# One load of x split between two DMA queues: 12 KB of fifteen rows through GpSimd's, 12 KB of a sixteenth in sixteen pieces

## The chip, the cores and the metric

The kernel runs on one core of a Trainium2 chip. The metric is the device time in microseconds (us) from launch to end; a time is the median of several executions, and one further execution was recorded by the hardware profiler. Lower is better.

## What is computed

The reference is a low-rank update of a residual stream. Input `x` has 16 x 512 = 8192 tokens of 768 float32 values, `A` is 768 x 16, `B` is 16 x 768:

```python
lora = np.matmul(np.matmul(x, A), B)
return (x + scale * lora).astype(np.float32)   # scale = 0.5
```

So 25.2 MB of `x` have to be read and 25.2 MB of output written; `A` and `B` are 48 KB each.

## The kernel before, in words

**Tiling.** The tokens lie in five parts of 8, 8, 16, 16 and 16 tokens per partition (`PARTS`, L14); a part of S tokens takes S x 128 rows of `x`, and partition p holds S rows that follow one another in memory. A partition's share of one load is therefore one run of bytes, 3 KB per token: 48 KB for the load of a part of 16. All of `x` but the last part has its own room in on-chip memory (`x_all`, L62); the last part takes the room of the first two, once these are stored. The result is summed into `x_all` in place and stored from there.

**Loads and stores.** `LOADS` (L106) cuts the five parts into eight loads, numbered 0 to 7; `STORES` (L129) has five. All of them, and those of `A` (three DMAs of four rows of 4 KB, L156) and `B` (one DMA of 16 rows of 3 KB, L160), are issued by SyncE (`on_sync`, L136), in this order: loads 0 and 1, `A`, `B`, loads 2 to 5; then stores 0 and 1; load 6 when store 0 has landed, load 7 when store 1 has landed; then stores 2 and 3, and store 4 at L356. Before store 2 SyncE waits until TensorE has begun its sixth pass over `raised(0)` (`s_raise`, L182). Each load has a semaphore of its own (`s_load`), which reaches 16 when all of the load has landed. **Load 5** is the one that the change touches: part 3, 16 tokens, 6144 KB, 48 KB on each of the 128 partitions. It is the largest of the loads.

**Compute.** Tokens go in groups of 8 (`GROUP`), half a group (`SUB` = 4) at a time through the narrowing to float16 (`narrowed`, L188): ScalarE takes the first half of every group, GpSimd the second. VectorE transposes the group in 32 x 32 blocks (L255), TensorE multiplies by `A` (L285), ScalarE spreads the product into a block-diagonal tile (`y_bd`, L240), TensorE multiplies by `B` (L306), and VectorE adds the product to `x` in place (L260), two tokens at a time. The engines' programs are written out by hand, with semaphores; nothing is planned by a scheduler inside this section.

**GpSimd** (`on_gpsimd`, L200) begins with memsets and the mask `pick`, narrows the first two tokens of group 0 (load 0), waits for `B` (L213), narrows it (`b_half`, L214), waits for the transposed `A`, and builds the weights (`w_one`, `w_bd`, L216 to L225). Then it narrows the second half of groups 1 to 7 (L226). Group 4 is tokens 0 to 7 of load 5, group 5 its tokens 8 to 15; GpSimd reads tokens 12 to 15 of it in group 5.

Of the kernel before, what the change touches and what calls it, by code (L numbers as in the profile page):

```python
# [16 lines left out]
GROUP = 8  # L17

SUB = 4
# [9 lines left out]
def kernel(  # L29
# [9 lines left out]
    fp32 = mybir.dt.float32  # L39
    P = 128  # L40
# [3 lines left out]
    x2 = x.flatten_outer_dims()  # L44
# [10 lines left out]
    def sb(name, shape, dtype):  # L55
        return nc.alloc_sbuf_tensor(name, shape, dtype).ap()

    def ps(name, shape):
        return nc.alloc_psum_tensor(name, shape, fp32).ap()
# [15 lines left out]
    xn = sb("xn", [P, GROUP, D], MM_DT)  # L75
    xt = sb("xt", [P, GROUP, D], MM_DT)
    y_bd = sb("y_bd", [P, GROUP, P], MM_DT)
    lora = [ps(f"lora_ps{i}", [P, 2, D]) for i in range(2)]
    y_ps = ps("ps_yt", [P, GROUP, Q])

# [2 lines left out]
    def sem(name):  # L83
        sems.append(nc.alloc_semaphore(name))
        return sems[-1]
# [3 lines left out]
    where = []  # L89
# [6 lines left out]
    def memory(t2, i, s, n):  # L96
        S = PARTS[i]
        return t2[ds(parts[i], S * P), :].rearrange("(p s) d -> p s d", s=S)[:, ds(s, n), :]

    def held(i, s, n):  # L100
        return tiles(where.index((i, s)), n)

    def tiles(t, n):
        return x_all[:, ds(t % ROOM, n), :]

    LOADS = [  # L106
        (0, 0, 2), (0, 2, 6), (1, 0, 8), (2, 0, 8), (2, 8, 8), (3, 0, 16), (4, 0, 8), (4, 8, 8)
    ]
    s_load = [sem(f"s_load{k}") for k in range(len(LOADS))]

    def load_of(t):
        i, s = where[t]
        return next(k for k, ld in enumerate(LOADS) if ld[0] == i and ld[1] <= s < ld[1] + ld[2])
# [9 lines left out]
    s_out0, s_out1, s_raise = sem("s_out0"), sem("s_out1"), sem("s_raise")  # L123


    s_sum, s_out = tc.alloc_semaphore("s_sum"), tc.alloc_semaphore("s_out")

    MMS = 2 * NC
# [6 lines left out]

    def on_sync(e):  # L136
        def load(k):
            ld = LOADS[k]
            e.dma_start(out=held(*ld), in_=memory(x2, *ld)).then_inc(s_load[k], 16)  # L139

        def summed(k):
            e.wait_ge(s_sum, k + 1)
            if STORED[k] + 1 < NG:

                e.sem_inc(s_free[PAIRS - 1], 1)

        def store(k, done):
            st = STORES[k]
            e.dma_start(out=memory(out2, *st), in_=held(*st)).then_inc(done, 16)

        load(0)
        load(1)
        e.wait_ge(s_ready, 1)
        blocks = A.rearrange("(c e) r -> c (e r)", e=64)
        for c in range(SETS):
            e.dma_start(  # L156
                out=a_rows[c : SET * SET : SET, :], in_=blocks[ds(c * SET, SET), :]
            ).then_inc(s_a, 16)
        e.wait_ge(s_brows, 1)
        e.dma_start(out=b_rows[0 : R * APART : APART, :], in_=B).then_inc(s_b, 16)  # L160
        for k in range(2, len(LOADS) - 2):
            load(k)

        for p in range(2, PAIRS):
            e.sem_inc(s_free[p], 1)
        summed(0)
        summed(1)


        e.wait_ge(s_lora, 2 * PAIRS + 2)  # L170
        store(0, s_out0)
        store(1, s_out1)
        e.wait_ge(s_out0, 16)
        load(len(LOADS) - 2)
        e.wait_ge(s_out1, 16)
        load(len(LOADS) - 1)
        for k in range(2, len(STORES)):
            summed(k)
            if k == 2:


                e.wait_ge(s_raise, 6)  # L182
            if k + 1 < len(STORES):
                store(k, s_out)
# [3 lines left out]
    def narrowed(e, copy, g, first, n=SUB):  # L188
        t = g * GROUP + first
        for k in dict.fromkeys(load_of(t + k) for k in range(n)):  # L190
            if (e, k) not in here:
                here.add((e, k))
                e.wait_ge(s_load[k], 16)
        if g:
            e.wait_ge(s_taken, g)
        ins = copy(out=xn[:, ds(first, n), :], in_=tiles(t, n))  # L196

        ins.then_inc(s_narrow if g else s_first if first else s_a, 1)

    def on_gpsimd(e):  # L200
        e.memset(a_rows[0:Q], 0.0).then_inc(s_ready, 1)  # L201
        e.memset(b_rows, 0.0).then_inc(s_brows, 1)  # L202
        e.memset(pick, 0.0).then_inc(s_pick, 1)
        e.memset(w_bd.rearrange("p c k m -> p (c k m)").bitcast(fp32), 0.0)  # L204
        e.memset(y_bd.rearrange("p s m -> p (s m)").bitcast(fp32), 0.0).then_inc(s_ready, 1)  # L205
        e.wait_ge(s_pick, 1)
        e.affine_select(  # L207
            out=pick, in_=pick, compare_op=mybir.AluOpType.not_equal, fill=1.0, base=0,
            pattern=[[0, NQ], [-APART, Q]], channel_multiplier=1,
        ).then_inc(s_pick, 1)  # L210
        narrowed(e, e.tensor_copy, 0, 0, SUB // 2)
        e.wait_ge(s_pick, 2)
        e.wait_ge(s_b, 16)  # L213
        e.tensor_copy(out=b_half, in_=b_rows).then_inc(s_bh, 1)  # L214
        e.wait_ge(s_ready, 3)
        e.tensor_copy(  # L216
            out=w_one.rearrange("i (c e) k r -> i c e (k r)", c=SETS),
            in_=a_t[0:Q].rearrange("i k r (e c) -> i c e (k r)", c=SET)[:, 0:SETS, 0:SET, :],
        ).then_inc(s_w, 1)
        e.wait_ge(s_w, 1)  # L220
        for b in range(NQ):
            e.tensor_copy(  # L222
                out=w_bd[ds(b * Q, Q), :, :, ds(b * Q, R)], in_=w_one
            ).then_inc(s_w, 1)
            e.wait_ge(s_w, b + 2)  # L225
        for g in range(1, NG):  # L226
            narrowed(e, e.tensor_copy, g, SUB)

    def on_scalar(e):
        narrowed(e, e.copy, 0, SUB // 2, SUB // 2)  # L230
        narrowed(e, e.copy, 0, SUB)
        e.wait_ge(s_bp, 1)
        e.copy(out=b_mm, in_=lora[0][:, 0, :]).then_inc(s_bm, 1)  # L233
        for g in range(NG):
            if g + 1 < NG:
                narrowed(e, e.copy, g + 1, 0)
            e.wait_ge(s_y, g + 1)
            for b in range(NQ):
                q = ds(b * Q, Q)
                last = e.mul(out=y_bd[q, :, q], in_=y_ps[q, :, :], mul=sc)  # L240
                if b == 0 and g + 1 < NG:

                    last.then_inc(s_narrow, 1)
            last.then_inc(s_spread, 1)
# [93 lines left out]

    on_sync(nc.sync)
    on_gpsimd(nc.gpsimd)  # L340
    on_scalar(nc.scalar)
    on_vector(nc.vector)
# [53 lines left out]
```

## Time and profile before

| | us |
|---|---|
| median of three executions | 123.53 |
| lowest and highest of them | 123.52 and 123.67 |
| the profiled execution | 123.47 |
| span of its instructions on the core | 121.7 |

The profile shows five engines (PE = TensorE, DVE = VectorE, ACT = ScalarE, POOL = GpSimd, SP = SyncE) and the packets of sixteen DMA engines, which all queues share. In lists of instructions the columns are the start in us from the span's beginning, the duration in us, the engine, the source line, the operation, the written and the read tile, and in brackets the idle time before it and what ended that idle time. "DMA share" is the mean busy share of the sixteen DMA engines. The packet records of the trace give each packet's start, duration, size and queue, but not which of the sixteen engines carried it. A packet of 4 bytes is the closing one of a DMA on one engine: it raises the DMA's semaphore.

### The profile page before, as it was taken

How to read it: one execution, taken by the hardware profiler on the slowest of the kernel's cores; microseconds unless marked ns; L12 is line 12 of the kernel's file. 1: busy time of each engine (PE TensorE's matmuls, PEld its weight loads, DVE VectorE, ACT ScalarE, POOL GpSimd, SP SyncE). 2: the span in 40 equal slices, each digit the busy share in tenths (PEclk: the TensorE clock that was granted, in tenths of full speed). 3: DMA queues.
4: the chain of work that ended last, by engine and by line, in shares of the span. 5: the costliest groups of instructions: out<-in, count | busy, mean ns of one | idle time of the engine just before them, and what ended most of it. 6: DMA issues, size and time to landing. Idle time of an engine off the chain costs nothing.

```text
span 121.7 us, 889 instructions
## 1 busy us (share of the span) xinstructions
PE 50.7 (42%) x322; PEld 29.6 (24%) x322; DVE 81.7 (67%) x42; ACT 37.4 (31%) x43; POOL 28.4 (23%) x24
## 2 busy tenths in 40 slices
PE   0000239477457647745745744774674320000000
PEld 0000026243323424423423322442442110000000
DVE  0002850599999999999999989999995991000000
ACT  4003928526409313644440192733004000000000
POOL 7721638017009002604400170710000000000000
PEclk9999999999999999999999999999999995555555
DMA  3999999999998997999999999997998899799790
GB/s 65 442 418 440 444 420 428 444 420 428 477 517 355 420 517 307 452 412 436 452 396 428 460 404 436 469 517 323 452 517 388 388 517 436 339 517 452 323 517 0
DMA packets 1928, 50.43 MB, mean 414 GB/s; under 512 B 236, under 2 KB 236, under 8 KB 392
## 3 DMA queue, kind: packets, MB, share of 16 engines
q1 hardware_dynamic: 1928, 50.43, 97.0%
HBM read 25.26 MB, written 25.17 MB: 414 GB/s over the span
## 4 chain that ended last, share of the span: by engine, by line
DVE 34%; DMA 28%; PE 10%; ACT 9%; issue 1%; SPq 0%; POOLq 0%
DVE x_sb L260 22%; DMA x_sb<-in_x_dram 20%; DVE xt L255 12%; DMA out_dram<-x_sb 8%; PE ps_yt L285 6%; ACT xn L196 6%; PE lora_ps L306 3%; ACT y_bd L240 3%; SPq L139 0%; SPq L391 0%; POOLq L134 0%; POOLq L377 0%
## 5 line engine op out<-in xcount | busy, mean ns | idle before, releaser
L260 DVE TENSOR_TENSOR x_sb<-x_sb,lora_ps 128x1536 f32<-128x1536 f32 x32 | 53.7, 1734 | 1.4 <-PE lora_ps L306 1.4
L306 PE MATMUL lora_ps<-b_mm,y_bd 128*128 128x512 f16 (+1 forms) x128 | 25.0, 328 | 22.4 <-ACT y_bd L240 14.1
L196 ACT CAST xn<-x_sb 128x3072 f16<-128x3072 f32 (+1 forms) x9 | 23.4, 2609 | 35.4 <-DMA x_sb<-in_x_dram 25.7
L285 PE MATMUL ps_yt<-xt,w_bd 128*128 128x256 f16 x192 | 26.1, 288 | 12.7 <-DVE xt L255 12.7
L255 DVE STREAM_TRANSPOSE xt<-xn 128x3072 f32<-128x3072 f32 (+1 forms) x9 | 27.0, 3005 | 6.5 <-ACT y_bd L240 6.1
L196 POOL CAST xn<-x_sb 128x3072 f16<-128x3072 f32 (+1 forms) x8 | 20.7, 2586 | 44.7 <-DMA x_sb<-in_x_dram 26.2
L285 PEld LDWEIGHTS ps_yt<-xt,w_bd 128*128 128x128 f16 x192 | 18.9, 101 | 20.6 <-issue 15.8
L306 PEld LDWEIGHTS lora_ps<-b_mm,y_bd 128*128 128x128 f16 x128 | 10.6, 98 | 35.3 <-ACT y_bd L240 16.4
L240 ACT ACTIVATE y_bd<-ps_yt 32x256 f16<-32x256 f32 x32 | 12.0, 374 | 19.5 <-PE ps_yt L285 19.1
L248 DVE STREAM_TRANSPOSE a_t<-a_rows 32x1024 f32<-32x1024 f32 x1 | 1.9, 1943 | 11.3 <-DMA a_rows<-in_A_dram 11.3
L319 PE MATMUL lora_ps<-b_half,pick 128*128 128x512 f16 (+1 forms) x2 | 0.8, 500 | 12.5 <-POOL b_half L214 12.5
L319 PEld LDWEIGHTS lora_ps<-b_half,pick 128*128 128x128 f16 x2 | 0.1, 106 | 12.5 <-issue 12.5
L222 POOL COPY w_bd<-w_one 32x384 f16<-32x384 f16 x4 | 2.0, 499 | 0.2
L214 POOL CAST b_half<-b_rows 128x768 f16<-128x768 f32 x1 | 0.8, 827 | 4.6 <-DMA b_rows<-in_B_dram 4.6
L196 ACT ACT_TABLE_LOAD x1 | 1.3, 1283 | 0.9 <-PEq L377 0.9
L204 POOL MEMSET w_bd<- 128x1536 f32 x1 | 1.4, 1372 | 0.0
L201 POOL MEMSET a_rows<- 32x1024 f32 x1 | 0.9, 941 | 0.5 <-POOLq L134 0.5
L216 POOL CAST w_one<-a_t 32x384 f16<-32x384 f32 x1 | 0.8, 849 | 0.9 <-DVE a_t L248 0.9
L233 ACT CAST b_mm<-lora_ps 128x768 f16<-128x768 f32 x1 | 0.8, 798 | 0.0
L202 POOL MEMSET b_rows<- 128x768 f32 x1 | 0.7, 727 | 0.0
L205 POOL MEMSET y_bd<- 128x512 f32 x1 | 0.5, 514 | 0.0
L207 POOL TENSOR_SCALAR_AFFINE_SELECT pick<-pick 128x128 f16<-128x128 f16 x1 | 0.3, 298 | 0.0
(5 smaller groups left out, 0.6 us busy)
## 6 DMA issues: line engine op xcount, KB each, us to landing
out_dram<-x_sb SPq DMA_DIRECT2D x3, 6144.0 KB, 19.4
x_sb<-in_x_dram SPq DMA_DIRECT2D x5, 3072.0 KB, 14.6
x_sb<-in_x_dram SPq DMA_DIRECT2D x1, 6144.0 KB, 41.6
out_dram<-x_sb SPq DMA_DIRECT2D x2, 3072.0 KB, 13.8
x_sb<-in_x_dram SPq DMA_DIRECT2D x1, 2304.0 KB, 9.7
x_sb<-in_x_dram SPq DMA_DIRECT2D x1, 768.0 KB, 4.6
a_rows<-in_A_dram SPq DMA_DIRECT2D x3, 16.0 KB
b_rows<-in_B_dram SPq DMA_DIRECT2D x1, 48.0 KB, 7.5
```

The costliest lines, as they stand in the source:

```text
L196: ins = copy(out=xn[:, ds(first, n), :], in_=tiles(t, n))
L201: e.memset(a_rows[0:Q], 0.0).then_inc(s_ready, 1)
L204: e.memset(w_bd.rearrange("p c k m -> p (c k m)").bitcast(fp32), 0.0)
L214: e.tensor_copy(out=b_half, in_=b_rows).then_inc(s_bh, 1)
L222: e.tensor_copy(out=w_bd[ds(b * Q, Q), :, :, ds(b * Q, R)], in_=w_one).then_inc(s_w, 1)
L240: last = e.mul(out=y_bd[q, :, q], in_=y_ps[q, :, :], mul=sc)
L248: e.transpose(out=a_t[0:Q].rearrange("i k r c -> i (k r) c"), in_=a_rows[0:Q].rearrange("c (i k r) -> c (k r) i", k=2, r=R),).then_inc(s_r ...
L255: return e.transpose(out=ts[0], in_=ts[1])
L260: ins = e.tensor_tensor(out=xs, in0=xs, in1=lora[p % 2], op=mybir.AluOpType.add)
L285: mm = e.matmul(y_ps, w_bd[:, c, k, :], xv[:, :, c, :, k], start=(m == 0), stop=(m == MMS - 1),)
L306: mms.append(e.matmul(t[:, k, ds(n0, w)], y_bd[:, 2 * p + k, :], b_mm[:, ds(n0, w)], start=True, stop=True,))
L319: last = e.matmul(lora[0][:, 0, ds(n0, w)], pick.rearrange("p b r -> p (b r)"), b_half[:, ds(n0, w)], start=True, stop=True,)
```

## The change

Load 5 is issued as several DMAs in place of one.

- Through SyncE's queue, in place of the single DMA: partitions 0 to 111 with all 16 tokens (48 KB each); partitions 112 to 127 with tokens 0 to 11 (36 KB each); partition 127 with tokens 12 to 15 (12 KB, one run of memory that is cut into 16 pieces of 768 bytes). All three count on load 5's semaphore, so its readers wait for 48 and not for 16.
- Through GpSimd's queue, issued after GpSimd's first narrowing and before its wait for `B`: tokens 12 to 15 (12 KB each) of partitions 112 to 118, seven rows; then a single element into a spare tile that nothing reads; then the same tokens of partitions 119 to 126, eight rows. They count on a new semaphore `s_dealt`.
- GpSimd waits for `s_dealt` to reach 48 before it narrows the second half of group 5, the reader of tokens 12 to 15.

```diff
+    DEALT, CUT, FROM = 5, P - 16, 12
+    SHARES = [
+        (slice(0, CUT), slice(0, 16)), (slice(CUT, P), slice(0, FROM)),
+        (slice(P - 1, P), slice(FROM, 16)),
+    ]
+    DEALS = [slice(CUT, CUT + 7), None, slice(CUT + 7, P - 1)]
+    needs = {k: 16 for k in range(len(LOADS))}
+    needs[DEALT] = 16 * len(SHARES)
...
         def load(k):
-            ld = LOADS[k]
-            e.dma_start(out=held(*ld), in_=memory(x2, *ld)).then_inc(s_load[k], 16)
+            i, s, n = LOADS[k]
+            for rows, cols in SHARES if k == DEALT else [(slice(0, P), slice(0, n))]:
+                e.dma_start(
+                    out=held(i, s, n)[rows, cols], in_=memory(x2, i, s, n)[rows, cols]
+                ).then_inc(s_load[k], 16)
...
-                e.wait_ge(s_load[k], 16)
+                e.wait_ge(s_load[k], needs[k])
...
         narrowed(e, e.tensor_copy, 0, 0, SUB // 2)
+        ld = LOADS[DEALT]
+        for rows in DEALS:
+            to = held(*ld)[rows, FROM:] if rows else spare
+            of = memory(x2, *ld)[rows, FROM:] if rows else x2[0:1, 0:1]
+            e.dma_start(out=to, in_=of).then_inc(s_dealt, 16)
         e.wait_ge(s_pick, 2)
         e.wait_ge(s_b, 16)
...
         for g in range(1, NG):
+            if load_of(g * GROUP + SUB) == DEALT and where[g * GROUP + SUB][1] == FROM:
+                e.wait_ge(s_dealt, 16 * len(DEALS))
             narrowed(e, e.tensor_copy, g, SUB)
```

More of the change, by code (lines that the diff above doesn't have):

```diff
@@ L77 @@
     y_bd = sb("y_bd", [P, GROUP, P], MM_DT)
+    spare = sb("spare", [1, 1], fp32)
     lora = [ps(f"lora_ps{i}", [P, 2, D]) for i in range(2)]
@@ L123 @@
     s_out0, s_out1, s_raise = sem("s_out0"), sem("s_out1"), sem("s_raise")
+    s_dealt = tc.alloc_semaphore("s_dealt")
     s_sum, s_out = tc.alloc_semaphore("s_sum"), tc.alloc_semaphore("s_out")
```

## The prediction, made before the changed kernel ran

> **What bounds the kernel now.** I read the page first: the busy shares and the sixteen DMA engines.
>
> ```profile
> PE 50.7 (42%) x322; PEld 29.6 (24%) x322; DVE 81.7 (67%) x42; ACT 37.4 (31%) x43; POOL 28.4 (23%) x24
> ...
> DMA packets 1928, 50.43 MB, mean 414 GB/s; under 512 B 236, under 2 KB 236, under 8 KB 392
> ...
> q1 hardware_dynamic: 1928, 50.43, 97.0%
> ```
>
> No compute engine is near full. The DMA engines are: 97.0% of sixteen engines over 121.7 us, 118.0 us each for 3.15 MB. The page's chain of waits is 34% VectorE, and that misleads here: it names what came last before each issue, and an issue that finds transfers still queued delays nothing. So I looked, by stretches, for a place where the transfers run dry (columns: stretch, its length, busy time and count of each engine, TensorE's clock, DMA share, GB/s).
>
> ```profile
> 6.00:12.00 6.00, 0.00 (x0) 0.00 (x0) 0.72 (x1) 0.92 (x1) 1.40 (x2) 1.00 1.02 435
> 12.00:32.00 20.00, 11.89 (x66) 6.99 (x66) 13.92 (x8) 11.32 (x10) 8.74 (x8) 1.00 1.00 430
> 32.00:46.50 14.50, 7.82 (x52) 4.62 (x53) 14.50 (x8) 5.43 (x9) 2.75 (x1) 1.00 1.00 434
> ```
>
> The share is 1.0 throughout. The packet records confirm it: the next packet of an engine starts 3 to 4 ns before the last one ends, so the packets can be linked into sixteen chains, one per engine. No chain has a pause over 0.03 us between 3 us and the end, but two: 0.18 and 0.15 us at 75.9. Each chain carries the same bytes of `x`; four also carry the three 4 KB rows of `A`, so `A`'s four rows lie on four engines only.
>
> So the time is that of the engine that finishes last. Three windows of the DMA view, 119.38 to 119.93, 119.93 to 120.38 and 120.38 to the end, give the closing packets:
>
> ```profile
> DMA packets 15, 0.00 MB, mean 0 GB/s; under 512 B 15, under 2 KB 15, under 8 KB 15
> DMA packets 0, 0.00 MB, mean 0 GB/s; under 512 B 0, under 2 KB 0, under 8 KB 0
> DMA packets 1, 0.00 MB, mean 0 GB/s; under 512 B 1, under 2 KB 1, under 8 KB 1
> ```
>
> Fifteen engines close by 119.93, then comes half a microsecond with nothing, and **one engine closes last**, at 120.389. From the chains:
>
> ```
>             carries A   closes load 7   closes store 2   closes store 4
> slow engine    no           76.221          91.127          120.389
> next           yes          76.412          90.919          119.919
> others               75.876 to 76.374    to 90.877       to 119.877
> ```
>
> At load 7 it was in the pack. It loses 0.5 us after that: its 48 KB packets of stores 2 and 3 took 1.82 to 1.90 us where the others took 1.815. I don't know why.
>
> **The change part by part.**
>
> *Bytes.* I read 7 rows, one element, 8 rows as sixteen pieces dealt to sixteen engines in turn: fifteen engines get back the 12 KB that the 36 KB rows left out, and the eighth gets four bytes. The sixteenth row's 12 KB go to all, 768 bytes each. At the 435 GB/s of the first row above (27.2 per engine), 12 KB is 0.45 us. The small costs come from the records: one 48 KB packet takes 1815 ns, two of 24 KB take 912 each, so a cut costs 9; a closing packet takes 9; sizes from 3 KB (121 ns) up lie on a line of 8 ns plus 36.8 per KB (of 1000 bytes), which gives 36 for 768 bytes. Each engine gets two more closings on SyncE's queue and, I assume, three on GpSimd's: 45 ns.
> - Fifteen engines: 9 + 36 + 45 = **0.09 us more**.
> - The relieved engine: 0.45 less, 9 + 36 + 45 more: **0.36 us less**.
>
> [...]
>
> *What the relief is worth.* If the relieved engine is the slow one, it would close at 120.389 - 0.36 = 120.03, and the next at 119.919 + 0.09 = 120.01: a gain of 0.36. But it has to have work at 76, where two engines already ran dry. These are the DMA view's windows 75.8 to 76.06 and 76.05 to 76.07, and SyncE's list with the chain before it:
>
> ```profile
> DMA packets 8, 0.15 MB, mean 567 GB/s; under 512 B 5, under 2 KB 5, under 8 KB 5
> DMA packets 2, 0.10 MB, mean 4915 GB/s; under 512 B 0, under 2 KB 0, under 8 KB 0
> ```
> ```profile
> 74.41 0.34 SPq L149 DMA_DIRECT2D out_dram<-x_sb  x1
> ```
> ```profile
> 55.01 14.58 DMA x_sb<-in_x_dram
> 69.59 0.02 issue
> 69.61 2.75 ACT xn L196
> 72.36 0.02 issue
> 72.39 0.38 ACT y_bd L240
> ```
>
> By 76.06 five engines have closed load 7, but only three have begun store 2 (at 75.890 the first); two more begin at 76.06 without a closing beside them. Store 2 is issued at 74.41 and reaches an engine 1.48 to 1.65 us later. Its issue hangs on load 6 landing at 69.59, then 2.75 us of narrowing, then `y_bd`, then TensorE. The last closing of load 6 (69.107) is on an engine with `A` rows, not the slow one: it comes 0.09 later after the change, and so does store 2, which reaches the engines between 75.98 and 76.15. The slow engine's first packet of it started at 76.227; relieved, it would be ready at 75.87 and must wait. I take the middle, 76.065: it **keeps 0.16 of its 0.36 us** (0.08 to 0.25). The 44.2 us from there to its closing have no further gate: store 4 is issued at 101.51, and the slow engine closes store 3 at 105.857, the others by 105.419.
>
> *GpSimd's three issues.* They stand in this hole, 6.97 to 11.57:
>
> ```profile
> 5.51 1.46 POOL L196 CAST xn<-x_sb 128x1536 f16<-128x1536 f32 x1 [0.65 <-DMA x_sb<-in_x_dram]
> 11.57 0.83 POOL L214 CAST b_half<-b_rows 128x768 f16<-128x768 f32 x1 [4.60 <-DMA b_rows<-in_B_dram]
> 13.29 0.85 POOL L216 CAST w_one<-a_t 32x384 f16<-32x384 f32 x1 [0.89 <-DVE a_t L248]
> 14.20 2.18 POOL L222 COPY w_bd<-w_one 32x384 f16<-32x384 f16 x4
> 15.24 1.78 DVE L255 STREAM_TRANSPOSE xt<-xn 128x1536 f32<-128x1536 f32 x1 [0.35 <-ACT xn L196]
> 17.16 5.14 PE L285 MATMUL ps_yt<-xt,w_bd 128*128 128x256 f16 x24 [3.82 <-DVE xt L255]
> ```
>
> No row shows a DMA issue on GpSimd. The nearest are SyncE's, 0.34 to 0.75 us; the farthest is GpSimd's own longest instruction, 2.75. I take SyncE's 0.75 at most: 2.3 us of a hole of 4.60, so nothing. Without that cover `b_half`, `w_one` and `w_bd` are late; `w_bd` ends at 16.38, 0.65 before the transpose at 17.02 that TensorE needs too.
>
> *Order of arrival.* GpSimd's rows overtake: load 5 stood behind loads 1 to 4 in SyncE's queue, and its 12 KB now come some 30 us early, before load 1 has landed, or soon after. Load 1 feeds the first projection and lands at 11.06:
>
> ```profile
> 11.08 4.13 ACT L196 CAST xn<-x_sb 128x1536 f16<-128x1536 f32 x2 [8.91 <-DMA x_sb<-in_x_dram]
> 44.70 0.82 SPq L149 DMA_DIRECT2D out_dram<-x_sb  x2
> ```
>
> Up to 0.45 us late, it shifts compute up to store 0's issue at 44.70 by as much. That store is needed when an engine closes load 5, at 46.53 to 47.24 by the chains; with the 1.48 to 1.65 from above it arrives at 46.2 to 46.8. Some engines that are early anyway may pause; the ones that decide don't. From load 6 on compute follows the transfers again.
>
> *SyncE's two further issues* end near 7.8 us, and SyncE has nothing more to issue until 44.70. *GpSimd's new wait* stands before its narrowing of group 5, with groups 6 and 7 behind it; rows that come by 12 us are long there. The cost of both is nothing.
>
> *A second queue on an engine.* No row shows two queues in turn. From below nothing; from above one restart of a dry engine, the 0.18 us pause at 75.9. I take nothing, since between two loads of one queue no time is lost. A gain is excluded: an engine at its full rate can't be fed faster.
>
> **Sum.** Profiled 123.47 - 0.16 = 123.31. The median of the runs is 0.06 above the profiled execution: **123.37**.
>
> **Rivals.**
> - *Another engine is relieved.* The slow one pays 0.09, is in the pack at 76 and closes last: 123.62. For it: the records name no engine, and the change picks one by count. Against: four engines bear `A` and aren't slow, so the choice is among twelve.
> - *The gate at 76 lets the slow engine through.* It keeps nearly all of 0.36: 123.17. For it: one engine began store 2 as early as 75.890, and three of five without a pause. Against: that is still later than 75.87, and store 2 moves later with load 6.
> - *The rows aren't dealt in turn* (the change doesn't do what it says): 7 and 8 rows both start at the first engine, so seven engines carry 24 KB and eight none. Seven pay 0.45 + 0.09. If an `A` engine is among them it closes at 119.919 + 0.54 = 120.46, 0.07 later than now; if the slow one is among them, 0.54 later: 123.60 to 124.07. For it: `A`'s three DMAs of four rows all fell on the same four engines of SyncE's queue; were GpSimd's queue to do the same, it would go this way. [...]
> - *GpSimd's issues are long* (slower). At 2.75 us each, three take 8.25, the hole and the 0.65 cover 5.25, so TensorE's first projection is 3.0 late, store 0 comes 3.0 late, and every engine pauses some 2.3 us, as the engines that decide have about 0.7 to spare at 47: 125.8. It decides from (5.25 + 0.7) / 3 = 2.0 us per issue. Against: SyncE's issues take a quarter of that.
>
> **How the numbers follow.** That the relieved engine is the slow one lies between one in twelve (the engines without `A`) and certain, and the records don't tie the two or part them: I take the middle, 0.55. Chances: the forecast 0.45 (its own range 123.28 to 123.45) and the gate open 0.10 out of that; another engine 0.25; not dealt in turn 0.12; long issues 0.08. The forecast and the open gate alone can give more than 0.2% (0.25 us, about what a measurement of this kernel can tell from no change): the gate's 0.10 and as much again from the forecast's edge make faster 0.20. Slower by as much: long issues, the upper half of the rows not dealt in turn, and another engine relieved with the 0.18 of a second queue on top: 0.20. The rest, 0.60, is within 0.2%. The range runs from the open gate, 123.15, to another engine relieved with that 0.18, 123.80, with a little on it for the lower half of the rows not dealt in turn: 123.85. What is left out is the long issues and rows piled on the slow engine.
>
> **What would show it.** Three issues on GpSimd between 7 and 11.5, and fifteen 12 KB packets on a second queue soon after, on fifteen chains. At 76 the relieved chain pauses up to 0.28 us; if it is the slow one, the lone last closing comes nearer to the pack. A lone closing as far behind as before says that another engine was relieved. Two packets of 12 KB on one chain say that the rows weren't dealt. `b_half` starting after 11.6 by more than the shift of `B`'s landing says that the issues are long. The forecast is wrong if the slow engine's loss at 76 to 106 isn't tied to that engine, or if GpSimd's queue costs an engine more than its packets.

## The result, and the profile after

| | us |
|---|---|
| changed kernel, median of four (lowest, highest) | 142.06 (141.38, 142.79) |
| before, median of four on the same chip | 123.58 |
| ratio, 95% interval | 1.150 (1.143 to 1.157) |

The change costs 18.5 us, 15%. It was forecast within 0.2% of no change; none of the rivals comes near.

The page of the changed kernel answers to the lines of before, which showed 1928 packets, 414 GB/s and 97.0%. The GB/s row has forty slices of 3.5 us.

```profile
span 139.8 us, 895 instructions
...
DMA  4999999999998999978999999979979999999990
GB/s 102 450 415 267 387 302 415 422 436 436 331 267 225 324 253 236 116 190 355 415 436 408 443 422 422 422 316 450 450 309 408 450 450 450 450 436 450 450 436 28
DMA packets 2042, 50.43 MB, mean 361 GB/s; under 512 B 334, under 2 KB 334, under 8 KB 490
## 3 DMA queue, kind: packets, MB, share of 16 engines
q1 hardware_dynamic: 1946, 50.25, 95.6%
q0 software_dynamic: 96, 0.18, 0.6%
```

The engines are nearly as busy as before, 95.6% of a longer span, with the same bytes. Up to 90 us they don't run out of packets; they move them more slowly. The rate falls in two places: slices 3 to 5 (10 to 21 us) and 10 to 17 (35 to 63 us). It falls once more in slice 26 (91 to 94.5 us), but there the engines pause, as told below under the gate. In stretches chosen by the first two (columns as in the prediction):

```profile
6.00:11.00 5.00, 0.00 (x0) 0.00 (x0) 0.00 (x0) 0.00 (x0) 2.58 (x4) 1.00 1.03 434
11.00:18.00 7.00, 1.68 (x7) 0.79 (x8) 5.39 (x3) 4.92 (x3) 3.67 (x6) 1.00 1.08 302
18.00:33.00 15.00, 10.46 (x46) 6.07 (x45) 6.68 (x3) 6.91 (x6) 5.49 (x2) 0.77 0.97 405
33.00:38.00 5.00, 3.36 (x25) 2.05 (x22) 4.91 (x3) 1.50 (x4) 0.00 (x0) 1.00 1.18 369
38.00:57.00 19.00, 10.58 (x73) 6.39 (x72) 18.35 (x10) 4.25 (x5) 2.75 (x1) 1.00 1.05 257
57.00:66.00 9.00, 0.00 (x0) 0.00 (x0) 0.00 (x0) 0.00 (x0) 0.00 (x0) 0.65 0.80 214
66.00:92.00 26.00, 14.26 (x80) 8.41 (x80) 20.63 (x11) 12.23 (x14) 8.25 (x3) 0.79 0.98 416
```

A DMA share of 1.05 beside 257 GB/s, where before it was 1.00 beside 434: that pair says that each packet takes longer, not that packets are missing. ScalarE's list tells when the loads had landed, before (L196) and in the changed kernel (L213):

```profile
18.60 2.75 ACT L196 CAST xn<-x_sb 128x3072 f16<-128x3072 f32 x1 [2.57 <-DMA x_sb<-in_x_dram]
...
47.74 2.75 ACT L196 CAST xn<-x_sb 128x3072 f16<-128x3072 f32 x1 [4.59 <-DMA x_sb<-in_x_dram]
```
```profile
22.66 2.75 ACT L213 CAST xn<-x_sb 128x3072 f16<-128x3072 f32 x1 [6.68 <-DMA x_sb<-in_x_dram]
...
66.53 2.75 ACT L213 CAST xn<-x_sb 128x3072 f16<-128x3072 f32 x1 [19.63 <-DMA x_sb<-in_x_dram]
```

Load 2 is read at 22.66 (18.60 before), load 5 at 66.53 (47.74 before). The first 4.1 us arise while GpSimd's rows land, at 10.9 to 18.7; the rest, to 18.8, while load 5 does. After that nothing more is lost: the two profiled executions end 18.1 us apart. The packet records, by size:

```
                                                 before        changed
48 KB packets of load 5, median us (longest)     1.820 (1.84)  3.25 (5.12)
its 36 KB packets (sixteen rows)                 -             4.60 (5.10)
24 KB packets from 9.5 to 24 us over 1.0 us      0 of 245      48 of 185
  the longest                                    0.93          2.61
```

Two smaller findings stand in the issues of the changed kernel:

```profile
6.88 0.67 POOL L233 DMA_DIRECT2D x_sb<-in_x_dram  x1
7.55 0.52 POOL L233 DMA_DIRECT2D spare<-in_x_dram  x1
8.06 0.52 POOL L233 DMA_DIRECT2D x_sb<-in_x_dram  x1
```
```profile
x_sb<-in_x_dram SPq DMA_DIRECT2D x1, 12.0 KB
```

GpSimd's issues take 0.52 to 0.67 us. And the sixteenth row's 12 KB aren't cut: the records have one packet of 12 KB for them on SyncE's queue and none of 768 bytes. Where the description of the change and the prediction speak of sixteen pieces, one engine carried the row. Its packet took 1.06 us, from 64.87 to 65.94, and was the last of load 5: the 36 KB packets had ended by 65.15.

### The profile page after: what moved, and what is told of

Read it like the earlier page. It is cut to its first block, busy times and chain, and to the rows that moved or that the text cites. A ratio compares the mean times of both kernels' runs of the same rounds, so it can differ in the third digit from the quotient of the medians.

```text
span 139.8 us, 895 instructions
## 1 busy us (share of the span) xinstructions
PE 57.9 (41%) x322; PEld 33.4 (24%) x322; DVE 82.1 (59%) x42; ACT 37.4 (27%) x43; POOL 30.1 (22%) x27
## 3 DMA queue, kind: packets, MB, share of 16 engines
q1 hardware_dynamic: 1946, 50.25, 95.6%
## 4 chain that ended last, share of the span: by engine, by line
DMA 41%; DVE 22%; PE 12%; ACT 7%; SPq 2%; issue 1%; POOL 1%; POOLq 0%
DMA x_sb<-in_x_dram 23%; DMA out_dram<-x_sb 18%; DVE x_sb L284 14%; DVE xt L279 7%; PE lora_ps L330 6%; PE ps_yt L309 6%; ACT xn L213 4%; ACT y_bd L264 3%; SPq L173 1%; POOL a_rows L218 1%; SPq L177 0%; POOLq L415 0%; POOLq L401 0%; POOLq L148 0%
## 5 line engine op out<-in xcount | busy, mean ns | idle before, releaser
L330 PE MATMUL lora_ps<-b_mm,y_bd 128*128 128x512 f16 (+1 forms) x128 | 29.0, 370 | 37.1 <-ACT y_bd L264 31.5
L213 ACT CAST xn<-x_sb 128x3072 f16<-128x3072 f32 (+1 forms) x9 | 23.4, 2609 | 56.0 <-DMA x_sb<-in_x_dram 42.6
L309 PE MATMUL ps_yt<-xt,w_bd 128*128 128x256 f16 x192 | 30.3, 318 | 10.6 <-DVE xt L279 10.6
L213 POOL CAST xn<-x_sb 128x3072 f16<-128x3072 f32 (+1 forms) x8 | 20.7, 2588 | 63.5 <-DMA x_sb<-in_x_dram 41.7
L309 PEld LDWEIGHTS ps_yt<-xt,w_bd 128*128 128x128 f16 x192 | 20.9, 111 | 20.5 <-issue 13.8
L330 PEld LDWEIGHTS lora_ps<-b_mm,y_bd 128*128 128x128 f16 x128 | 12.4, 108 | 51.3 <-ACT y_bd L264 33.9
L264 ACT ACTIVATE y_bd<-ps_yt 32x256 f16<-32x256 f32 x32 | 12.0, 375 | 18.5 <-PE ps_yt L309 18.1
L233 POOL DMA_DIRECT2D x_sb<-in_x_dram x2 | 1.2, 596 | 0.0
L233 POOL DMA_DIRECT2D spare<-in_x_dram x1 | 0.5, 518 | 0.0
## 6 DMA issues: line engine op xcount, KB each, us to landing
x_sb<-in_x_dram SPq DMA_DIRECT2D x5, 3072.0 KB, 18.1
```

Of the source, the lines that this page charges most:

```text
L233: e.dma_start(out=to, in_=of).then_inc(s_dealt, 16)
L309: mm = e.matmul(y_ps, w_bd[:, c, k, :], xv[:, :, c, :, k], start=(m == 0), stop=(m == MMS - 1),)
L330: mms.append(e.matmul(t[:, k, ds(n0, w)], y_bd[:, 2 * p + k, :], b_mm[:, ds(n0, w)], start=True, stop=True,))
```

## The experiments

**Theory P.** How long a packet takes depends on which partitions the engines serve at the same moment. Load 5 as one DMA of 128 partitions has no long packet (48 KB in 1.82 us, 1.84 at most); where it is cut by partitions, and while the fifteen rows go to partitions 112 to 126, packets hold each other up (48 KB in 3.25 us, 24 KB in up to 2.61). If so, the cut alone costs what load 5 lost in the changed kernel (28.2 us from load 4's landing to its own, 14.5 before: 13.7) and a little for the 12 KB a row that come along, and the fifteen rows alone cost the 4.1 us that load 2 lost. Which other sets of partitions collide was the author's estimate; the runs measure it.

**Rivals.** Q: the second queue makes the DMA engines slow. N: the number of DMAs does. H: rows of memory 48 KB apart, read at once, collide on the memory's side.

**One part alone: the cut** (`cut_only`). GpSimd's DMAs go; load 5 is

```diff
+    SHARES = [(slice(0, 112), slice(0, 16)), (slice(112, 128), slice(0, 16))]
```

> Load 5 goes through SyncE's queue alone, as two DMAs: partitions 0 to 111 and partitions 112 to 127, all 16 tokens of each; GpSimd issues nothing. [...] Rival Q (a second queue on the DMA engines is what is slow): no second queue, 123.6. Rival N (more DMAs on SyncE's queue cost by their number): within 0.2 of 123.6.

Measured: 137.98 beside 123.47, +14.5 (ratio 1.117, 1.114 to 1.120), near P's 13.7 and a little. There is no second queue here, so Q is not the cause of these 14.5 us; and it is one DMA more, for which N had 0.2 us at most. The stretches of loads 2 to 4, of the 112 rows and of the sixteen:

```profile
12.00:32.00 20.00, 12.03 (x66) 6.99 (x66) 13.64 (x8) 11.19 (x10) 8.61 (x8) 1.00 1.02 434
33.00:54.00 21.00, 11.89 (x80) 7.09 (x80) 19.76 (x10) 4.63 (x7) 2.75 (x1) 1.00 0.98 236
54.00:60.00 6.00, 0.00 (x0) 0.00 (x0) 0.00 (x0) 0.00 (x0) 0.00 (x0) 0.73 0.82 115
```

434 GB/s, then 236, then 115. The sixteen rows get 115; a quarter of 434 is 109. Their 48 KB packets took 6.25 us in the median, 3.4 times the 1.82 of before. The 112 rows' took 3.32.

**The other part alone: the deal** (`deal_only`). Load 5 stays whole; GpSimd's three DMAs fill a tile that nothing reads (`ld` is part 3, tokens 12 to 15).

```diff
+        for to, rows in [(slice(112, 119), slice(112, 119)), (None, None), (slice(119, 127), slice(119, 127))]:
+            out = other[to] if rows else spare
+            of = memory(x2, *ld)[rows] if rows else x2[0:1, 0:1]
+            e.dma_start(out=out, in_=of).then_inc(s_dealt, 16)
...
```

> Load 5 stays one DMA. GpSimd issues its three DMAs at the same place, but into a tile of their own at the same partitions 112 to 126 (the data is read a second time, 180 KB, and nothing uses it). [...] Rival Q: nearly all of the 18.5 us, 138 to 142. Rival N: 124.0, the bytes alone.

Measured: 127.45 beside 123.47, +4.0 (1.032, 1.029 to 1.035), P's 4.1. So 14.5 + 4.0 is the whole 18.5. The two runs are not quite the changed kernel's halves: in `cut_only` the sixteen rows carry 48 KB and not 36 (6.25 us a packet where the changed kernel has 4.60), and the 12 KB row that ended load 5 there is missing. That these differences cancel is not shown by a run of its own. While the seven rows land the rate halves, comes back, and falls again with the eight:

```profile
10.50:13.50 3.00, 0.00 (x0) 0.00 (x0) 2.12 (x2) 2.49 (x2) 0.30 (x1) 1.00 0.97 213
13.50:15.50 2.00, 0.80 (x2) 0.14 (x2) 1.80 (x2) 1.98 (x2) 1.87 (x4) 1.00 1.02 424
15.50:18.50 3.00, 1.33 (x7) 0.95 (x8) 1.45 (x1) 0.46 (x1) 1.44 (x3) 1.00 1.14 299
```

**The same rows of memory to other partitions** (`deal_spread`, its edit beside `deal_only`), which parts P from H and Q; that partitions 0 to 24 and 64 to 92 don't collide was the author's estimate:

```diff
-        for to, rows in [(slice(112, 119), slice(112, 119)), (None, None), (slice(119, 127), slice(119, 127))]:
+        for to, rows in [(slice(0, 28, 4), slice(112, 119)), (None, None), (slice(64, 96, 4), slice(119, 127))]:
```

> [...] Theory P: the rows cost only their bytes, 0.45 us on fifteen engines: 123.9 to 124.3, and 24 KB packets beside them take 1.4 us at most where they took up to 2.6. Rival Q, and rival H (rows of memory 48 KB apart that are read at once collide there): the same time as with the rows at partitions 112 to 126.

Measured: 125.13, +1.7 (1.013, 1.011 to 1.015). The same reads, the same queue, 2.3 us less than with the rows at partitions 112 to 126: Q and H, which forecast the same time as there, fall. But P as I had put it asked for +0.45 to +0.8. The stretches and the packets say why:

```profile
10.50:13.50 3.00, 0.80 (x2) 0.14 (x2) 2.41 (x2) 2.31 (x2) 1.21 (x2) 1.00 0.96 409
13.50:15.00 1.50, 0.00 (x0) 0.00 (x0) 1.21 (x1) 1.50 (x1) 1.37 (x3) 1.00 1.13 442
15.00:17.50 2.50, 0.23 (x2) 0.20 (x3) 1.78 (x1) 1.11 (x2) 1.09 (x3) 1.00 0.93 285
```
```
                24 KB packets over 1.0 us   GpSimd's 12 KB packets, us
                (longest)                   first DMA        second DMA
deal_only       61 (2.61)                   0.47 to 1.28     0.47 to 1.02
deal_spread     28 (1.63)                   0.46 to 0.47     0.47 to 0.77
deal_owner      0 (0.93)                    0.46 to 0.47     0.46 to 0.47
deal_fifteen    0 (0.98)                    0.46 to 0.48     -
```

The first seven rows disturbed nobody, the second eight did. Linked into chains between 10 and 18.5 us, GpSimd's packets fell twice on the same seven engines, and the eighth packet of the second DMA on one more; eight engines got none. So both DMAs begin at the same engine: the rows are not dealt in turn. The number of packets, which needs no linking, agrees that each DMA is laid out over all sixteen engines: GpSimd's three DMAs left 96 packets, two for each engine and DMA. These are 15 rows, the element, 48 closings, and 32 more of 4 bytes: as many as there are engines without a row or the element, counted over the three DMAs. The seven rows were written to partitions 0 to 24, the eight to 64 to 92: rows that are spread can collide too.

**The eight rows to other partitions** (`deal_owner`): they go to `slice(32, 64, 4)`, all else as in `deal_spread`. That rows at partitions 32 to 60 don't collide was the author's estimate.

> [...] If so, no 24 KB packet outside is stretched and the 12 KB packets of both DMAs take 0.46 to 0.48: two rows on each of seven engines, 0.9 us more, 124.3 to 124.6. [...]

Measured: 124.39 beside 123.55, +0.84 (1.008, 1.006 to 1.009), as expected. The second stretch that was slow is gone:

```profile
10.50:13.50 3.00, 0.00 (x0) 0.02 (x1) 1.43 (x1) 2.44 (x2) 0.83 (x1) 1.00 1.08 458
13.50:15.00 1.50, 0.80 (x2) 0.12 (x2) 1.50 (x2) 1.50 (x1) 0.85 (x2) 1.00 0.91 385
15.00:17.50 2.50, 0.02 (x1) 0.05 (x2) 2.34 (x2) 0.98 (x2) 1.99 (x4) 1.00 1.03 442
```

What is left is two rows on each of seven engines, 0.92 us. The two runs differ only in where the eight rows are written: with 64 to 92 the 24 KB packets took up to 1.63 us, with 32 to 60 up to 0.93. What sets these partitions apart isn't shown.

**One DMA of fifteen rows** (`deal_fifteen`) in GpSimd's queue in place of three, to partitions 32, 36 to 88:

```diff
+        for to, rows in [(slice(32, 92, 4), slice(112, 127))]:
```

If fifteen engines bear one row each, the rows cost one 12 KB packet, 0.46 to 0.47 us in `deal_owner`.

> [...] If fifteen rows go to fewer engines (five with three rows each, or one), 0.9 to 1.4 us or more.

Measured: 124.19 beside 123.39, +0.80 (1.006, 1.005 to 1.008). Fifteen chains have one 12 KB packet each and the sixteenth none, each 0.46 to 0.48: one row to an engine. The time is 0.3 us more than such a packet. The records show it within load 5, whose packets on most engines lose 0.2 to 1.2 us in all, and not beside GpSimd's rows. Twenty-two of its 48 KB packets are over 1.86 us; before there are none, but `store_middle`, which changes nothing up to store 2, has five. Why stays open.

**Load 5 in halves** (`halves`) **and with a whole middle** (`middle_half`), on SyncE's queue alone:

```diff
+    SHARES = [(slice(0, 64), slice(0, 16)), (slice(64, 128), slice(0, 16))]
```
```diff
+    SHARES = [(slice(32, 96), slice(0, 16)), (slice(0, 32), slice(0, 16)), (slice(96, 128), slice(0, 16))]
```

> Load 5 as two DMAs through SyncE's queue, partitions 0 to 63 and 64 to 127, all 16 tokens. [...] Rival H (rows of memory of one pitch read at once collide): the same pitch and count as the middle half, so 1.82 us a packet and 123.6.

> Load 5 as three DMAs through SyncE's queue: partitions 32 to 95, then 0 to 31, then 96 to 127, all 16 tokens. [...] Rival H: the three DMAs read rows of the same pitch, so their packets take the same time, be it 1.8 or 3.3. Rival N: within 0.2 of 123.6.

Measured: 139.47 for the halves in one execution, +15.9 over 123.55; 131.40 for the middle, +7.9 (1.064, 1.061 to 1.067) over 123.47. All are on one queue, with the same size of row; the first two lines are one kernel, the third is `halves`:

```
48 KB packets, us                10th     median   90th of a hundred
partitions 32 to 95               1.815    1.820    1.827
partitions 0 to 31, 96 to 127     3.524    3.819    3.854
partitions 0 to 63, 64 to 127     3.649    3.838    3.849
```

The middle runs at full rate though it is cut out (1.82 us a packet); the halves, of the same number of rows, at half or less (3.84; 175 GB/s of 434 in either half, from 33.0 to 46.5 and from 48.5 to 62.0 us). H, which asked for 1.82 in the halves too, falls again. It isn't the number of partitions that counts, then, but which they are; why 32 to 95 differ from 0 to 63 is not shown. The middle kernel's stretches, with the middle first:

```profile
33.00:39.00 6.00, 3.67 (x25) 2.09 (x24) 6.00 (x4) 2.75 (x1) 2.75 (x1) 1.00 0.91 393
41.00:47.00 6.00, 3.27 (x22) 1.96 (x23) 6.00 (x4) 1.15 (x4) 0.00 (x0) 1.00 0.99 205
```

**A cut that leaves all partitions together** (`token_cut`):

```diff
+    SHARES = [(slice(0, 128), slice(0, 12)), (slice(0, 128), slice(12, 16))]
```

> Load 5 as two DMAs through SyncE's queue of all 128 partitions each: tokens 0 to 11, then 12 to 15. [...] Rival N (cutting a load costs by itself): more than 0.3 us.

Measured: 123.66 beside 123.55 (1.001, 1.000 to 1.002): 0.1, about the 0.08 of eight more packets and one closing to an engine, 9 ns each as in the prediction. N falls for good.

**The same cut on a store** (`store_middle`): store 2 as partitions 32 to 95, 0 to 31 and 96 to 127. Load 5 cut so cost 7.9 us; does it matter which partitions are served when they are read, too?

> Loads as before, nothing on GpSimd's queue. Store 2 (16 tokens, 48 KB a partition) as three DMAs: partitions 32 to 95, 0 to 31, 96 to 127. [...]

Measured: 131.33 beside 123.39, +7.9 (1.064, 1.062 to 1.066). Its 48 KB packets took 1.82 us in the middle and 3.79 in the rest: the partitions decide when they are read as well as when they are written.

**An attempt to relieve engines without a cut** (`a_twelve`):

```diff
-        for c in range(SETS):
-            e.dma_start(
-                out=a_rows[c : SET * SET : SET, :], in_=blocks[ds(c * SET, SET), :]
-            ).then_inc(s_a, 16)
+        e.dma_start(out=a_rows[0 : Q * SETS : Q // SET, :], in_=blocks).then_inc(s_a, 16)
...
```

> Not a part of the change: load 5 as before, nothing on GpSimd's queue. A's twelve rows come in one DMA, to partitions 0, 8 to 88, in place of three DMAs of four rows, so that twelve engines bear 4 KB each and not four 12 KB; VectorE transposes three quadrants in place of one and GpSimd makes w_one in three copies. In the packets linked anew the four engines with A are among the last, the lone last one too. If the last engine sets the time: 0.32 us off these four, 0.16 on eight others, whose last then closes some 0.15 later than before, and store 2 reaches the engines no earlier than load 6's last closing allows: 0.1 to 0.3 us faster, 123.2 to 123.4. If the lone last engine isn't one of the four: 0 to 0.16 slower.

Measured: 123.93 beside 123.55, slower by 0.4 (1.004, 1.002 to 1.005); 0.1 to 0.3 faster was expected. The stretch in which `A` lands and the one after it fell to 424 and 430 GB/s,

```profile
6.00:12.00 6.00, 0.00 (x0) 0.00 (x0) 0.53 (x1) 0.67 (x1) 1.25 (x2) 1.00 1.03 424
12.00:20.00 8.00, 3.38 (x15) 1.93 (x16) 4.88 (x3) 5.42 (x4) 4.88 (x9) 1.00 1.00 430
```

from 435 (in the prediction) and 436 before:

```profile
12.00:20.00 8.00, 3.63 (x16) 2.11 (x17) 4.67 (x3) 5.40 (x4) 4.56 (x7) 1.00 1.02 436
```

P suggests itself, but the packets don't show it: the twelve 4 KB packets of `A` took 0.16 us each, as before (one 0.19). What took longer are sixteen 24 KB packets that run side by side right behind, from 10.2 to 10.9 on, so one on each engine: 1.07 to 1.14 us where 0.91 is usual. That is 0.2 us on every engine, half of the loss. Its cause stays open.

No kernel here beats the one before, so it stays.

## Why the prediction was wrong, point by point

**What bounds the kernel** held: sixteen DMA engines, and the one that finishes last. In the changed kernel the engines that close last don't pause either, so nearly all of what slows the packets comes out in the time: 18.8 us when load 5 is read, 18.1 at the end of the profiled execution.

**The step that failed is "Bytes"**: "Fifteen engines: 9 + 36 + 45 = 0.09 us more" and "The relieved engine: ... 0.36 us less". It priced a piece by its bytes at 27.2 GB/s per engine, a rate that before shows for DMAs of 128 partitions and for the 3 and 4 KB rows of `A` and `B`, never for long rows on part of the partitions. Such a trace can't price another shape; the prediction should have set the range wide there. Two prices took the place of 0.09: the cut of load 5 cost 14.5 us (48 KB packets of 3.32 and 6.25 us for 1.82), GpSimd's rows 4.0 (24 KB packets up to 2.61 us for 0.92). The sixteenth row, priced at 36 ns on every engine, was 1.06 us on one.

**"Dealt to sixteen engines in turn"** failed as well. Linked in `deal_spread` and `deal_owner`, where the packets are stretched little or not at all, seven engines bore 24 KB through GpSimd's queue, one 12, eight none; the changed kernel issues the same three DMAs and has the same 96 packets. No run shows a dealing that goes on from one DMA to the next, on which the 0.36 us of relief and the forecast's 0.16 stood: in `deal_spread` and `deal_owner` the seven and the eight rows begin at the same engine, and in `deal_fifteen` fifteen rows fall on fifteen engines. The rival by which the rows aren't dealt in turn had the dealing right. It priced it at 0.1 to 0.5, net of the 12 KB that every engine is spared in load 5. `deal_owner`, where nothing is spared, cost 0.84, and 0.84 less 0.45 is 0.39 (an estimate), so that price was fair for rows that don't collide; here they collided.

**The lone last engine.** By the closing packets, one engine closes last and alone, by 0.34 to 0.70 us, in the changed kernel and in four of the others, as before (0.47); in the remaining six the last two close within 0.15 us. The prediction's table has the lone engine of before without `A`'s rows. Linked anew with another rule, the records of before gave it `A`'s rows, those of `token_cut` didn't: two chains whose packets end within a few nanoseconds can be swapped, so that column proves nothing. Which engine it is stays open, and with it whether any dealing could relieve it.

**The gate at 76 us** moved to 93.9 in the changed kernel and held up more engines than before. Store 2 was issued at 93.01, 18.6 us later, and by then most engines had nothing left to do:

```profile
90.50:92.00 1.50, 0.00 (x0) 0.00 (x0) 0.72 (x2) 1.44 (x4) 0.49 (x1) 1.00 0.65 279
92.00:93.00 1.00, 0.41 (x3) 0.28 (x4) 1.00 (x1) 0.52 (x2) 0.00 (x0) 1.00 0.29 123
93.00:93.80 0.80, 0.80 (x7) 0.42 (x5) 0.80 (x1) 0.00 (x0) 0.00 (x0) 1.00 0.22 92
```

Linked into chains, thirteen engines paused there, 0.4 to 3.5 us; the three that didn't are those that closed last. So load 5's delay fell unevenly on the engines, and the early ones lost their lead at store 2. In `deal_owner` nine engines, most of them without GpSimd's rows, paused 0.2 to 0.7 us at 76: engines that are ahead do wait for store 2, as the prediction had it.

**GpSimd's issues** were right: 0.52 to 0.67 us each where 0.75 was the bound taken, and `b_half` wasn't late:

```profile
11.46 0.83 POOL L236 CAST b_half<-b_rows 128x768 f16<-128x768 f32 x1 [2.89 <-DMA b_rows<-in_B_dram]
```

**Order of arrival**: load 1 wasn't delayed (read at 11.03, 11.08 before); the rows came at 10.9, just behind it. **The second queue** cost nothing of its own: in `deal_owner` a 12 KB packet takes 0.46 us between two 24 KB packets that follow without a pause.

**The range and the slower rival.** The dearest rival was long issues; its price, 2.3 us, was an eighth of the loss, by another mechanism.

## What to carry to other kernels

In these runs a DMA's rate depended on which partitions its engines served at the same moment (48 KB packets of 1.82, 3.84 and 6.25 us), and the trace of before, with its DMAs of 128 partitions, said nothing of it. Cut a transfer along the free dimension, which cost 0.1 us here, and not by partitions, which cost 8 to 16; if partitions must be cut, 32 to 95 ran at full rate and 0 to 63 at half. Where the DMA share stays at 1.0 and the GB/s fall, look at packet durations before counting packets.

## What the runs showed of the hardware that was not expected

- Seven 12 KB rows to partitions 112 to 118 held up the packets of load 2 too: in `deal_only` at 10.5 to 13.5 us the sixteen engines together moved 213 GB/s of 434. That the target partitions decide is shown (409 in the same stretch of `deal_spread`); how seven rows slow all engines isn't.
- TensorE was slower behind some of the longer waits. In the changed kernel the eight matmuls of two `raised` calls took 2.74 us, where they took 1.47 before. Its granted clock in these stretches (26.90 to 29.70, and 23.90 to 25.50 before) was 0.50, and 1.00 before. That the wait is the reason was not tested:

```profile
23.95 1.47 PE L306 MATMUL lora_ps<-b_mm,y_bd 128*128 128x512 f16 x8 [1.64 <-ACT y_bd L240]
```
```profile
26.92 2.74 PE L330 MATMUL lora_ps<-b_mm,y_bd 128*128 128x512 f16 x8 [4.54 <-ACT y_bd L264]
```
